# Queries, key copies and a gate product in the first block of a two-block transformer kernel

## The chip, the cores and the metric

One core of one Trainium2 chip runs the whole program. The metric is the device time of one execution in microseconds, as the median over runs.

## What is computed

The reference runs two different two-layer blocks over 256 tokens of width 1024, everything in float32. The change touches the first block alone. One of its layers normalizes the input and projects it to ten parts: queries, keys, values and a gate for attention A (16 heads of 64, a mixture of dilated bands), the same for attention B (8 heads of differential attention), and two output gates. Cut to what matters here:

```python
qa, ka, va, za, qb, kb, vb, zb, ga, gb = split_cols(rms_norm(x) @ w_in)
qa, ka = partial_rope(qa), partial_rope(ka)          # first 16 of 64 columns of a head
ya = dilated_mixture(qa, ka, va) * silu(za)
qb, kb = partial_rope(qb), partial_rope(kb)
yb = subln(diff_attention(qb, kb, vb, lam)) * silu(zb)
x = x + (sigmoid(ga) * (ya @ w_proj_a) + sigmoid(gb) * (yb @ w_proj_b)) @ w_out
```

## The kernel before

Every large product is made in three matmuls per block (`mm3`): both operands are split into a high and a low part. A weight piece (128x1024) is loaded by SP (`raw`), its high part is made on ACT (`hi`), its low part on DVE (`lo`); four split pieces and three raw ones are held. A projection (`proj`) computes 256x512 outputs from four pieces: 16 blocks of three matmuls, eight row chunks by two halves t of the tokens. With `sweep`, all of half 0 comes before half 1; only the first group of a layer does that.

The order of all other work on the engines is written by a small planner. It has a clock that advances by 0.5 at each block (so a *step* of 1.0 is two blocks, six matmuls), and `at(k, fn)` issues `fn` once the clock has gone k steps further. Each engine runs its instructions in the order in which they were issued so, and waits for the semaphores of what it needs.

A layer of the first block makes four groups of eight heads' columns: two for attention A, two for attention B. Per group `qkv` projects queries, keys and values; `attend_a` or `attend_b` then puts the stages of all its heads on the planner, and these run beside the gate's projection and beside the next group's `qkv`. So the queries of the first group have no attention beside them, those of the second and third have attention A's, those of the fourth have attention B's.

Queries and keys leave PSUM through `turned`: ACT copies the half to `tok`, POOL turns its first 16 columns in four operations (`rope`), and `lag` steps later `flip` has PE transpose `tok` in four blocks. The queries' `then` (in `into_stack`) copies each of two row halves on ACT and subtracts on DVE; ACT's second copy and DVE's first subtraction write the same rows and take turns. The keys' `then` (in `into_keys`) does the same into `kh` and `kl`, and at the end four DMAs on SP's queue (`twin`) copy `kh` and `kl` to the other 64 rows. Heads with even number need the first `kh` and the first `kl` copy, the odd ones the second. SP's queue also carries the weight loads.

Attention A handles a head in stages: s (four score matmuls on PE; `s` and its maximum on DVE; `nm`, the scale, on POOL), e (`e`, exponentials on ACT), c (`pc`, the masked product, on DVE in two parts), t (three transposes `pt` on PE, copied by ACT), v (the product with the values into `o`). Behind the fourth and the eighth head follow the reciprocal `rd` on DVE, `rdh` on POOL, the scaled output `yo` on DVE, and the gate product into `sz`. Heads follow each other by 3.2 steps. PSUM buffers for scores, transposes and flips are three in rotation.

Of the kernel before, what the change touches and what calls it, by code (L numbers as in the profile page):

```python
# [16 lines left out]
ALU = mybir.AluOpType  # L17
# [60 lines left out]
def body(ctx: ExitStack, tc: tile.TileContext, I, out, upto=None):  # L78
    nc = tc.nc
    V, S, G, T = nc.vector, nc.scalar, nc.gpsimd, nc.tensor  # L80
# [22 lines left out]
    def tb_(name):  # L103
        o, n = _WHERE[name]
        return tab[:, o - n0:o - n0 + n]
# [118 lines left out]
    rope1 = (tb_("cc").rearrange("p (t d) -> p t d", t=2), tb_("ss").rearrange("p (t d) -> p t d", t=2))  # L224
# [16 lines left out]
    def tick(n=1.0):  # L241
        feed()
        pump(clk[0] + n)
# [54 lines left out]
    def piece():  # L298
        if not splits:
            feed()  # L300
        return splits.popleft()

    def release():
        count["done"] += 1

    def acc2():
        return [ps.tile([128, 512], F32, name="acc", tag="acc", bufs=4) for _ in range(2)]

    def mm3(a, n, lh, c, t, hi, lo, cc, first, last):
        sl = slice(t * 128, (t + 1) * 128)  # L310
        a = a[:, :n]
        T.matmul(a, lh[0][:, c, sl], hi[:, cc, :n], start=first, stop=False)  # L312
        T.matmul(a, lh[0][:, c, sl], lo[:, cc, :n], start=False, stop=False)  # L313
        T.matmul(a, lh[1][:, c, sl], hi[:, cc, :n], start=False, stop=last)  # L314

    def proj(lh, evac, sweep=False):

        acc = acc2()
        if not sweep:
            for c in range(8):  # L320
                if c % 2 == 0:
                    hi, lo, n = piece()
                for t in range(2):
                    mm3(acc[t], n, lh, c, t, hi, lo, c % 2, c == 0, c == 7)
                    if t and c % 2:
                        release()
                    if c == 7:
                        evac(acc[t], t)
                    tick(0.5)
        else:  # L330
            pieces = []
            for t in range(2):
                for c in range(8):
                    if t == 0 and c % 2 == 0:
                        pieces.append(piece())
                    hi, lo, n = pieces[c // 2]
                    mm3(acc[t], n, lh, c, t, hi, lo, c % 2, c == 0, c == 7)
                    if t and c % 2:
                        release()
                    if c == 7:  # L340
                        evac(acc[t], t)
                    tick(0.5)
# [92 lines left out]
    def turned(r, tabs, then, lag):  # L435

        tok = t4k("tok")

        def evac(acc, t):
            S.activation(tok[:, t, :], acc, AF.Copy, scale=factor(r, t))  # L440
            rope(tok[:, t, :], 8, tabs[0][:, t, :], tabs[1][:, t, :])

            def flip():
                p = wk([128, 4, 128], "tp")
                for a in range(4):
                    T.transpose(p[:, a, :], tok[:, t, a * 128:(a + 1) * 128], ident)
                then(p, slice(t * 128, t * 128 + 128), t)
            at(lag, flip)
        return tok, evac

    def halves(i):
        return slice(64 * i, 64 * i + 64), slice(64 - 64 * i, 128 - 64 * i)

    def into_stack(dst, r, tabs):


        def then(p, cols, t):
            for i in range(2):
                a, b = halves(i)
                h = dst[a, i:8:2, cols]  # L460
                S.activation(h, p[a], AF.Copy)
                V.tensor_tensor(out=dst[b, i:8:2, cols], in0=p[a], in1=h.bitcast(F32), op=ALU.subtract)
        return turned(r, tabs, then, 4)

    def into_keys(st, r, tabs):

        def then(p, cols, t):
            if t == 0:
                st["kh"] = act.tile([128, 8, 256], F32R, name="kh", tag="LT", bufs=1)
                st["kl"] = [act.tile([128, 4, 256], F32R, name="kl", tag="Y", bufs=2) for _ in range(2)]  # L470
            for i in range(2):
                a, _ = halves(i)
                h = st["kh"][a, i:8:2, cols]
                S.activation(h, p[a], AF.Copy)
                V.tensor_tensor(out=st["kl"][i][a, :, cols], in0=p[a], in1=h.bitcast(F32), op=ALU.subtract)
            if t == 1:
                def twin():
                    for i in range(2):
                        a, b = halves(i)
                        nc.sync.dma_start(st["kh"][b, i:8:2, :].bitcast(F32), st["kh"][a, i:8:2, :].bitcast(F32))  # L480
                    for i in range(2):
                        a, b = halves(i)
                        nc.sync.dma_start(st["kl"][i][b].bitcast(F32), st["kl"][i][a].bitcast(F32))
                at(0, twin)
        return turned(r, tabs, then, 5.3)[1]
# [135 lines left out]
    def layer1(l, last):  # L621
        lh, r, hr = nxt["lh"], nxt["r"], nxt["hr"]
# [10 lines left out]
        def attend_a(q, k, v, sz, la, g):  # L633
            st = {}

            def s_(h):
                if h % 4 == 0:
                    st["den", h // 4] = tiny(8, "den")
                s, mx = scores(q[:, h, :], k["kh"][:, h, :], k["kl"][h % 2][:, h // 2, :], tb_("ba"))
                nm = tiny(2, "nm")  # L640
                G.tensor_scalar(nm, mx, -0.125, None, op0=ALU.mult)
                st["s", h] = s, nm

            def e_(h):
                s, nm = st.pop(("s", h))
                e = e_tile()
                for j, (a, b) in enumerate(SPL):
                    S.activation(e[:, a:b], s[:, a:b], AF.Exp, bias=nm[:, j:j + 1], scale=0.125)
                st["e", h] = e

            def c_(h):
                den, i, e = st["den", h // 4], h % 4, st.pop(("e", h))
                pc = sm.tile([128, 384], F32, name="pc", tag="pc", bufs=2)
                for j, (a, b) in enumerate(SPL):
                    V.scalar_tensor_tensor(pc[:, a:b], e[:, a:b], 1.0, tb_("ca")[:, a:b], op0=ALU.mult,
                                           op1=ALU.mult, accum_out=den[:, 2 * i + 1 - j:2 * i + 2 - j])
                st["p", h] = pc

            def t_(h):
                st["pt", h] = probs_T(st.pop(("p", h)))  # L660

            def v_(h):
                hh, i = h // 4, h % 4
                if i == 0:
                    st["o"] = wk([128, 4, 2, 64], "o", "o", 1)
                o = st["o"]
                pv_mm(o[:, i, 1, :], o[:, i, 0, :], st.pop(("pt", h)), v, slice(64 * h, 64 * h + 64))
                if i < 3:
                    return
                rd = tiny(8, "rd")  # L670
                V.reciprocal(rd, st["den", hh])
                rdh = tiny(8, "rdh")
                for t in range(2):
                    G.tensor_scalar(by_block(rdh)[:, :, t], by_block(rd)[:, :, t], hr[:, t:t + 1], None, op0=ALU.mult)
                y = half_tile("yo").rearrange("p (t h d) -> p t h d", t=2, h=4)
                V.tensor_tensor(out=y, in0=o.rearrange("p h t d -> p t h d"),
                                in1=rdh.rearrange("p (h t) -> p t h", t=2)[:, :, :, None].to_broadcast([128, 2, 4, 64]),
                                op=ALU.mult)
                z = sz[:, :, 256 * hh:256 * hh + 256]
                G.tensor_tensor(out=z, in0=y.rearrange("p t h d -> p t (h d)"), in1=z, op=ALU.mult)  # L680
                if hh == 1:
                    for t in range(2):
                        at(3.5 + t, lambda t=t: to_lh(la, sz[:, t, :], 4 * g, t))

            for h in range(8):
                queue(3.2, [(d, lambda h=h, fn=fn: fn(h)) for d, fn in
                            ((-0.6, s_), (0.9, e_), (1.1, c_), (3.5, t_), (9.8, v_))])
# [62 lines left out]

        def qkv(first=False):
            q, k = qk_tile([8, 256], F32R), {}
            proj(lh, into_stack(q, r, rope1)[1], sweep=first)
            proj(lh, into_keys(k, r, rope1))
            v = t4k("R", "v")
            proj(lh, into_scaled(v, r))
            return q, k, v

        la = None
        for g in range(2):  # L760
            q, k, v = qkv(g == 0)
# [6 lines left out]
        for g in range(2):  # L768
            q, k, v = qkv()
# [725 lines left out]
    p = wk([128, 512])  # L1495
# [50 lines left out]
```

## Time and profile before

| | us |
|---|---|
| median of three runs | 1749.18 (1749.03 to 1752.28) |
| the profiled execution | 1747.13 |
| its span, first to last instruction | 1745.2 |
| PE busy in the span | 1709.6 |
| mean granted clock of PE | 0.993 of full |

Times within the trace count from the first instruction. A wait is idle time of an engine that ends with the event named. Matmuls overlap: a row's duration is longer than the distance to the next row, and the distance from start to start is what PE spends.

### The profile page before, as it was taken

How to read it: one execution, taken by the hardware profiler on the slowest of the kernel's cores; microseconds unless marked ns; L12 is line 12 of the kernel's file. 1: busy time of each engine (PE TensorE's matmuls, PEld its weight loads, DVE VectorE, ACT ScalarE, POOL GpSimd, SP SyncE). 2: the span in 40 equal slices, each digit the busy share in tenths (PEclk: the TensorE clock that was granted, in tenths of full speed). 3: DMA queues.
4: the chain of work that ended last, by engine and by line, in shares of the span. 5: the costliest groups of instructions: out<-in, count | busy, mean ns of one | idle time of the engine just before them, and what ended most of it. 6: DMA issues, size and time to landing. Idle time of an engine off the chain costs nothing.

```text
span 1745.2 us, 26891 instructions
## 1 busy us (share of the span) xinstructions
PE 1709.6 (98%) x9865; PEld 1485.3 (85%) x9865; DVE 1162.5 (67%) x2109; ACT 1013.2 (58%) x1834; POOL 329.2 (19%) x555
## 2 busy tenths in 40 slices
PE   8999999999999999999999999999999999999998
PEld 7788888888888888898889889998898888889997
DVE  5676776666767666779575676555778685675554
ACT  5666665466666654665676455445665666464443
POOL 2122421031224200342230000000442230010000
PEclk8999999999999999999999999999999999999999
DMA  6655565566554655555233555665555242646664
GB/s 206 195 163 160 158 192 169 168 192 183 169 156 147 192 178 174 169 169 136 88 103 97 186 175 183 191 185 169 170 158 150 76 114 86 198 157 197 184 184 143
DMA packets 158932, 282.27 MB, mean 162 GB/s; under 512 B 20560, under 2 KB 28496, under 8 KB 158800
## 3 DMA queue, kind: packets, MB, share of 16 engines
q1 hardware_dynamic: 157840, 277.83, 52.9%
q0 software_dynamic: 720, 2.62, 0.5%
q8 instruction: 78, 1.28, 0.3%
q14 instruction: 54, 0.44, 0.1%
q10 hardware_dynamic: 240, 0.09, 0.0%
HBM read 270.53 MB, written 1.59 MB: 156 GB/s over the span
## 4 chain that ended last, share of the span: by engine, by line
PE 48%; DVE 6%; ACT 2%; DMA 1%; issue 1%; POOL 0%; DVEq 0%; POOLq 0%; SPq 0%; ACTq 0%
PE acc L314 6%; PE acc L312 6%; PE acc L313 6%; PE acc L353 4%; PE acc L354 4%; PE acc L355 4%; PE facc L313 3%; PE facc L312 3%; PE facc L314 3%; DVE lo L285 2%; PE inv L1178 1%; PE inv L1168 1%; PE tp L371 1%; ACT hi L284 1%; PE pt L507 1%
## 5 line engine op out<-in xcount | busy, mean ns | idle before, releaser
L285 DVE TENSOR_TENSOR lo<-raw,hi 128x1024 fp32r<-128x1024 f32 (+1 forms) x504 | 621.7, 1240 | 339.7 <-ACT hi L284 322.5
L284 ACT ACTIVATE hi<-raw 128x1024 fp32r<-128x1024 f32 (+1 forms) x504 | 528.0, 1053 | 343.6 <-PE acc L314 139.8
L312 PE MATMUL acc<-hi,lhi 128*128 128x512 f32 (+1 forms) x1344 | 551.2, 410 | 2.5 <-ACT lhi L385 2.5
L314 PE MATMUL acc<-hi,llo 128*128 128x512 f32 (+1 forms) x1344 | 526.3, 392 | 0.5 <-DVE llo L388 0.3
L313 PE MATMUL acc<-lo,lhi 128*128 128x512 f32 (+1 forms) x1344 | 524.9, 391 | 0.5 <-DVE lo L285 0.4
L314 PEld LDWEIGHTS acc<-hi,llo 128*128 128x128 f32 x1344 | 253.9, 189 | 57.6 <-DVE llo L388 3.6
L313 PEld LDWEIGHTS acc<-lo,lhi 128*128 128x128 f32 x1344 | 255.6, 190 | 41.5 <-DVE lo L285 2.3
L312 PEld LDWEIGHTS acc<-hi,lhi 128*128 128x128 f32 x1344 | 255.7, 190 | 41.3 <-ACT lhi L385 2.8
L353 PE MATMUL acc<-lhi,hi 128*128 128x256 f32 x832 | 239.0, 287 | 0.0
L355 PE MATMUL acc<-lhi,lo 128*128 128x256 f32 x832 | 235.3, 283 | 0.0
L354 PE MATMUL acc<-llo,hi 128*128 128x256 f32 x832 | 235.2, 283 | 0.0
L353 PEld LDWEIGHTS acc<-lhi,hi 128*128 128x128 f32 x832 | 159.5, 192 | 1.2 <-issue 0.4
L354 PEld LDWEIGHTS acc<-llo,hi 128*128 128x128 f32 x832 | 159.4, 192 | 0.7
L355 PEld LDWEIGHTS acc<-lhi,lo 128*128 128x128 f32 x832 | 159.2, 191 | 0.0
L312 PE MATMUL facc<-hi,fh 128*128 128x512 f32 x256 | 99.8, 390 | 0.0
L313 PE MATMUL facc<-lo,fh 128*128 128x512 f32 x256 | 99.8, 390 | 0.0
L314 PE MATMUL facc<-hi,fl 128*128 128x512 f32 x256 | 99.6, 389 | 0.0
L546 POOL TENSOR_SCALAR pf<-pss 128x1 f32<-128x1 f32 x8 | 3.7, 459 | 468.0 <-ACT pj L856 468.0
L509 ACT ACTIVATE ptS<-pt 128x384 f32<-128x384 f32 x80 | 39.4, 492 | 83.0 <-PE pt L507 82.7
L500 DVE CUSTOM_DVE_ANT_0 s<-sc,tab 128x256 f32<-128x256 f32 x192 | 60.4, 351 | 10.7 <-PE sc L496 9.9
L314 PEld LDWEIGHTS facc<-hi,fl 128*128 128x128 f32 x256 | 48.1, 188 | 10.0
L312 PEld LDWEIGHTS facc<-hi,fh 128*128 128x128 f32 x256 | 48.1, 188 | 9.6
(309 smaller groups left out, 2299.3 us busy)
## 6 DMA issues: line engine op xcount, KB each, us to landing
raw<-in_w_in_dram SPq DMA_DIRECT2D x272, 512.0 KB, 3.7
raw<-in_w_ff_dram SPq DMA_DIRECT2D x128, 512.0 KB, 4.3
raw<-in_w_proj_a_dram SPq DMA_DIRECT2D x16, 512.0 KB, 4.2
raw<-in_w_proj_b_dram SPq DMA_DIRECT2D x16, 512.0 KB, 3.7
raw<-in_w_out_dram SPq DMA_DIRECT2D x16, 512.0 KB, 3.7
raw<-in_w_up_sw_dram SPq DMA_DIRECT2D x16, 512.0 KB, 3.6
raw<-in_w_up_dn_dram SPq DMA_DIRECT2D x16, 512.0 KB, 3.8
raw<-in_w_o_dram SPq DMA_DIRECT2D x16, 512.0 KB, 3.7
```

The source lines that it names most:

```text
L284: S.activation(hi[:, :, :o], raw[:, :, :o], AF.Copy)
L285: V.tensor_tensor(out=lo[:, :, :o], in0=raw[:, :, :o], in1=hi[:, :, :o].bitcast(F32), op=ALU.subtract)
L312: T.matmul(a, lh[0][:, c, sl], hi[:, cc, :n], start=first, stop=False)
L313: T.matmul(a, lh[0][:, c, sl], lo[:, cc, :n], start=False, stop=False)
L314: T.matmul(a, lh[1][:, c, sl], hi[:, cc, :n], start=False, stop=last)
L353: T.matmul(a, hi[:, c % 2, sl], lh[0][:, c, :], start=(c == 0 and m % 2 == 0), stop=False)
L354: T.matmul(a, hi[:, c % 2, sl], lh[1][:, c, :], start=False, stop=False)
L355: T.matmul(a, lo[:, c % 2, sl], lh[0][:, c, :], start=False, stop=(c == 7 and m % 2 == 1))
L371: T.transpose(p[:, a, :], src[:, a * 128:(a + 1) * 128], ident)
L500: V.tensor_tensor_reduce(s[:, a:b], sc[:, a:b], bias[:, a:b], 1.0, FMIN, ALU.add, ALU.max, accum_out=mx[:, j:j + 1])
L507: T.transpose(pt[:, j * 128:(j + 1) * 128], p[:, j * 128:(j + 1) * 128], ident)
L509: S.activation(r, pt, AF.Copy)
```

## The change

Three edits, all in the first block. The query flips are issued six steps behind their evacuation and no longer four, in all four groups of both layers (second block unchanged). The four key copies are issued as kh, kl for the even heads, then kh, kl for the odd ones. The gate product of attention A goes from POOL to DVE.

```diff
-    def into_stack(dst, r, tabs):
+    def into_stack(dst, r, tabs, lag=4):
...
-        return turned(r, tabs, then, 4)
+        return turned(r, tabs, then, lag)
...
                     for i in range(2):
                         a, b = halves(i)
                         nc.sync.dma_start(st["kh"][b, i:8:2, :].bitcast(F32), st["kh"][a, i:8:2, :].bitcast(F32))
-                    for i in range(2):
-                        a, b = halves(i)
                         nc.sync.dma_start(st["kl"][i][b].bitcast(F32), st["kl"][i][a].bitcast(F32))
...
                 z = sz[:, :, 256 * hh:256 * hh + 256]
-                G.tensor_tensor(out=z, in0=y.rearrange("p t h d -> p t (h d)"), in1=z, op=ALU.mult)
+                V.tensor_tensor(out=z, in0=y.rearrange("p t h d -> p t (h d)"), in1=z, op=ALU.mult)
...
             q, k = qk_tile([8, 256], F32R), {}
-            proj(lh, into_stack(q, r, rope1)[1], sweep=first)
+            proj(lh, into_stack(q, r, rope1, 6)[1], sweep=first)
```

## Rows read from the trace of the kernel before

**Rows 1.** The page, busy us, share of the span and instructions of each engine.

```profile
PE 1709.6 (98%) x9865; PEld 1485.3 (85%) x9865; DVE 1162.5 (67%) x2109; ACT 1013.2 (58%) x1834; POOL 329.2 (19%) x555
```

**Rows 2.** PE's waits by releaser, whole span: us in total, times, longest us.

```profile
PE pt L507 <- DVE pc L655: 3.0, 4, 0.8
PE sc L496 <- DMA kl<-kl: 3.0, 3, 1.5
...
PE tp L446 <- POOL tok L430: 2.5, 2, 2.0
```

**Rows 3.** Timeline of PE: start, us, instruction, count [idle before it <- releaser].

```profile
23.26 0.39 PE L314 MATMUL acc<-hi,llo 128*128 128x512 f32 x1
25.69 1.08 PE L446 MATMUL tp<-ident,tok 128*128 128x128 f32 x4 [2.04 <-POOL tok L430]
...
29.40 0.40 PE L313 MATMUL acc<-lo,lhi 128*128 128x512 f32 x1
...
33.28 0.60 PE L446 MATMUL tp<-ident,tok 128*128 128x128 f32 x4
...
35.33 0.39 PE L313 MATMUL acc<-lo,lhi 128*128 128x512 f32 x1
```

**Rows 4.** Windows: busy us of PE, PEld, DVE, ACT, POOL, PEclk, DMA share, GB/s.

```profile
25.70:29.30 3.60, 3.60 (x11) 3.03 (x12) 1.21 (x2) 1.72 (x3) 0.00 (x0) 0.53 0.84 294
59.00:62.00 3.00, 2.98 (x15) 2.52 (x16) 0.71 (x5) 0.71 (x1) 0.23 (x1) 1.00 1.04 349
```

**Rows 5.** Timeline of all engines, the first group's keys.

```profile
51.10 1.41 DVE L475 TENSOR_TENSOR kl<-tp,kh 64x512 fp32r<-64x512 f32 x2 [0.66 <-ACT kh L474]
51.71 2.05 SPq L480 DMA_DIRECT2D kh<-kh  x2
52.55 0.59 ACT L474 ACTIVATE kh<-tp 64x512 fp32r<-64x512 f32 x1 [0.86 <-DVE kl L475]
...
53.81 1.59 SPq L483 DMA_DIRECT2D kl<-kl  x2
...
59.02 0.36 PE L496 MATMUL sc<-kl,qk 128*128 128x256 f32 x1 [1.50 <-DMA kl<-kl]
```

**Rows 6.** Timeline of all engines, first attention A, sixth and seventh head.

```profile
94.03 0.42 DVE L655 SCALAR_TENSOR_TENSOR pc<-e,tab 128x256 f32<-128x256 f32 x1
...
96.30 0.43 DVE L500 CUSTOM_DVE_ANT_0 s<-sc,tab 128x256 f32<-128x256 f32 x1
...
99.38 0.69 DVE L676 TENSOR_TENSOR yo<-o,rdh 128x512 f32<-128x512 f32 x1 [2.32 <-POOL rdh L674]
...
99.99 1.22 DVE L285 TENSOR_TENSOR lo<-raw,hi 128x1024 fp32r<-128x1024 f32 x1
...
100.15 2.17 POOL L680 TENSOR_TENSOR sz<-yo,sz 128x512 f32<-128x512 f32 x1 [0.81 <-DVE yo L676]
...
101.12 1.49 DVE L655 SCALAR_TENSOR_TENSOR pc<-e,tab 128x256 f32<-128x256 f32 x1
...
102.54 0.53 DVE L655 SCALAR_TENSOR_TENSOR pc<-e,tab 128x128 f32<-128x128 f32 x1
102.67 0.79 PE L507 MATMUL pt<-ident,pc 128*128 128x128 f32 x3 [0.72 <-DVE pc L655]
```

**Rows 7.** Timeline of all engines, the second group's query flips.

```profile
89.06 0.69 DVE L462 TENSOR_TENSOR qk<-tp,qk 64x512 fp32r<-64x512 f32 x1 [0.66 <-ACT qk L461]
...
89.90 0.52 PE L507 MATMUL pt<-ident,pc 128*128 128x128 f32 x3
...
91.81 0.69 DVE L462 TENSOR_TENSOR qk<-tp,qk 64x512 fp32r<-64x512 f32 x1 [0.66 <-ACT qk L461]
...
93.27 0.79 ACT L648 ACTIVATE e<-s,nm 128x256 f32<-128x256 f32 x2
```

**Rows 8.** The page's costliest groups: busy us, mean ns | idle before, releaser.

```profile
L284 ACT ACTIVATE hi<-raw 128x1024 fp32r<-128x1024 f32 (+1 forms) x504 | 528.0, 1053 | 343.6 <-PE acc L314 139.8
```

**Rows 9.** Timeline of all engines, attention B's output beside the fourth group's keys.

```profile
213.95 0.35 DVE L743 SCALAR_TENSOR_TENSOR sz<-o,fh,sz 128x128 f32<-128x128 f32 x1 [2.12 <-POOL fh L738]
```

## The prediction

> **What bounds the kernel now.** I read the busy times first: PE is busy for 1709.6 of 1745.2 us, so only PE's waits can be won [rows 1]. Its waits by releaser came next. Three lines lie in the stages that the diff touches: 3.0 us in four waits of the probability transposes (pt) for the masked product pc, 3.0 us in three waits of the score matmuls for the copies of kl, 2.5 us in two waits of the token transposes for POOL's rotary embedding [rows 2]. That is 8.5 us, and the first flip costs more than its idle time shows. The flip of the first group's queries starts at 25.69; the last matmul before it was issued at 23.26, and the next would have followed 0.23 us later, at 23.49. From there to 29.40 PE does four transposes and seven matmuls. The second flip's four transposes and the seven matmuls behind them take 35.33 - 33.28 = 2.05 us [rows 3]. So the wait costs 29.40 - 23.49 - 2.05 = 3.86 us, 2.04 of it idle; the rest is the granted clock, 0.53 from 25.7 to 29.3, that is, mostly the 1.2 GHz level. After the 1.50 us wait at 59.02 it stays at 1.00 [rows 4].
>
> **The change part by part.**
>
> *Queries transposed two steps later, where they waited.* Two steps hold four blocks of three matmuls, 12 x 0.23 = 2.7 us, which is more than the 2.04 us wait. The embedding releases the flip at 25.69 as before, since POOL's order ahead of it is the same, and PE comes there at about 26.2. The key matmuls that now run ahead of the flip need two split weight pieces, which ACT and DVE made without PE's flip. So -3.86 us; the other flip wait, 2.5 - 2.04, goes too: -0.4 us. Kept at both ends of my range.
>
> *Key copies.* SP issues the four copies in program order. The second kh copy can't go before the last ACT copy, 52.55 + 0.59 = 53.14, so the first kl copy goes at 53.81, although DVE had finished its source at 51.10 + 1.41 = 52.51 [rows 5]. In the new order it goes at about 52.5, 1.3 us earlier, and with one copy of 256 KB less ahead of it. What waits for it, the first head's score at 59.02, had waited 1.50 us; the other two waits share 1.5 us. I take all 3.0 us as won (least: 2.4, if the landing moves only by the issue in the longest wait). The second kh copy goes about 0.7 us later; the second head's score is 3.2 steps behind the first's, at least 3.2 x 6 x 0.23 = 4.4 us, which hides it.
>
> *Gate product on DVE.* It runs eight times, twice per call of `attend_a`. The one behind the fourth head is beside a PE wait. POOL's product takes 2.17 us there, and DVE's first pc beside it takes 1.49 us instead of 0.42: 1.07 us lost on the path to the transposes at 102.67 [rows 6]. On DVE the product costs about half of a split's 1.22 us (128x512 for 128x1024, the same operation): 0.61 us, in the same queue ahead of the same pc. That gains 0.46. But POOL then starts the second half's four rotary operations as soon as rdh is done, beside product, split and pc. The second part of pc, with half the elements of the first, takes 0.53 us where one of them runs beside it, some 0.2 more than it should; two such meetings give nearly all of the gain back, one gives half. I take -0.25, between -0.5 and +0.5, for each of four windows: -1.0. The Trainium skill ("SBUF - State Buffer", Who interferes with whom) says that a DVE operation with two SBUF inputs and a GpSimd operation that reads SBUF exclude each other for the whole instruction; the 1.49 us agrees. By that rule the four rotary operations, which POOL works off ahead of rdh between s and yo, some 1.5 us together, could all fall in DVE's way, 1.0 us more than the product's move gains; the sum below would then be some 5 us higher, 1752, at the upper edge of no change, and its chance is in that case. The other four products stand behind the eighth head, where PE has no such wait: 0, hidden by DVE's idle third.
>
> *Queries transposed two steps later, where they did not wait.* The shift holds for all eight groups, and six of them have the previous group's attention running beside them. More than PE's transposes moves: each flip brings two ACT copies (0.6 us, as for the keys [rows 5]) and two DVE subtractions (0.69) that wait for each other in turn, and holds up what is queued behind them on ACT and DVE [rows 7]. In the second group they now end at 91.81 + 0.69 = 92.50, then come two weight splits, the sixth head's pc between them at 94.03, and the seventh head's score evacuation s at 96.30 [rows 6]. After the change the first split and the sixth head's exponential go ahead of the flips, the flips stand directly before the second split. The fifth head's transposes, now at 89.90, come at about 88.9 without two flips of 0.36 us ahead of them; behind them stand the copy of their result (some 0.5 us) and the exponential (0.79), so ACT turns to the flips at about 90.5. One flip takes 2 x (0.6 + 0.69) and the handovers, 2.7 us; pc comes between the two, 0.6; the second takes 2.0, as its first copy runs beside DVE's work for the first: 5.3 us, to 95.8. ACT is through its last copy 0.7 us earlier, at 95.1; its half of the split (1.05) [rows 8] ends at 96.1, DVE's (1.22) at about 97.3. So s comes about 1.0 us later. Nothing behind it has slack: s, its scale on POOL, the first half's embedding on POOL, rdh, then yo, for which DVE sat idle for 2.32 us, split, pc, and the transposes at 102.67 that PE already waits for. So they start 1.0 us later, in each of four windows: +4.0 us, bounds 0 (the chain catches up) and +6 (1.5 each, if ACT's handovers are slower). The idle time there grows a little more than that: the fifth head's transposes at 89.90 start right after the flip's subtraction at 89.06 frees their buffer, and no longer have to [rows 7], so PE comes some 0.25 us earlier.
>
> The last group of each layer has the other attention beside it. There the output scaling waits 2.12 us on DVE for POOL [rows 9], and the subtractions, which stood ahead of it, now stand behind it; the third head's exponentials, its transposes and the key flips follow. No row prices that; the nearest is those 2.12 us: between 0 and +2.1 in each of two windows, I take the middle: +2.0 together.
>
> *Sum*: -3.9 - 0.4 - 3.0 - 1.0 + 4.0 + 2.0 = -2.3 us. The profiled execution took 1747.13 us, so 1744.8; the median of the runs shown lies 2.05 us above it (1749.18), which gives about **1747 us**. Less than 0.2% (3.5 us) can't be told from no change here.
>
> **The rivals.** *The later flips cost little.* The chain could catch up before the seventh head's transposes, because ACT and DVE have idle time (DVE a third). Then the gains stand alone: -8.3 us, 1741. For it: the won waits are in the trace, the loss is not. Against: the chain to 102.67 runs through two in-order queues without a gap. It decides when the loss of the moved flips is under 4.8 us in all (I have 6.0).
>
> *The clock falls with the longer wait.* This one ends on the other side. The wait of the seventh head's transposes grows from 0.75 us (3.0 in four [rows 2]) to about 2.0 (0.75 + 1.0 + 0.25). Behind 2.04 us the clock fell, behind 1.50 it did not [rows 3 to 5]. A fall costs 3.86 - 2.04 = 1.8 us. In all four windows: 4 x 1.8 = 7.2, and -2.3 + 7.2 = +4.9 us, 1754; it decides from four falls on, or three with half a microsecond of other loss. For it: the row at 25.7; against: the estimate lies between the two waits that the trace shows, and four of four would have to fall. The Trainium skill ("TensorE: Matmul & The Clock Gate", Part 1: The HAM clock gate) says that the clock is gated by how busy PE has been and knows two levels; the row at 25.7 agrees.
>
> *The change does nothing for the copies*, because the landing is set by other transfers: DMA share is 1.04 from 59 to 62 [rows 4]. Then +3.0 on the sum, 1750, still no change.
>
> **How the numbers follow.** Losses of 4.8 to 11.8 us against 8.3 won: within 0.2%, chance 0.45 (the copies that don't help among them), and in its middle the forecast, 1747, own range 1745.7 to 1752.7. Losses under 4.8: faster, 0.33, since 6.0 is taken between wide bounds and lies only 1.2 above the line. Losses over 11.8, by the clock: slower, 0.22. The range for 8 in 10 reaches from the gains alone, 1741, to all four falls, 1754.
>
> **What would show it.** Right: no wait before the first flip and clock 1.00 from 20 to 40 us; no wait for kl; pc beside no POOL product at 0.42; but waits of pt for pc of 1.5 to 2.2 us, four times, s of the seventh head about 1 us later against the score on PE, and new waits in the last group of each layer. Wrong: pt waits no longer than 0.8 us (then the first rival), a granted clock of about 0.5 behind them (the second), or a wait for split weights behind 25 us.

## The result and the profile after

The changed kernel takes 1762.33 us (median of 6 runs, 1757.82 to 1767.89) against 1750.84 (6 runs of the kernel before, 1749.03 to 1752.28): ratio 1.0067, 95% interval 1.0053 to 1.0080. It is 11.7 us slower (9.3 to 14.0); no change was forecast, at -2.3 us. Below, a ratio is turned into us of 1750. The ratios are those on record, taken over the runs of both kernels; they need not equal the quotient of the two medians beside them (for e14 1.0018 against 1.0009). Line numbers behind line 481 are two lower than before, since the diff takes two lines away.

First the page's busy times of the changed kernel, then PE's waits over its whole span (us in total, times, longest); they answer to [rows 1, 2].

```profile
PE 1710.7 (97%) x9865; PEld 1483.5 (84%) x9865; DVE 1163.6 (66%) x2117; ACT 1010.9 (57%) x1834; POOL 317.2 (18%) x547
```

```profile
PE pt L505 <- DVE pc L653: 6.9, 5, 1.7
...
PE pt L505 <- DVE pc L714: 4.2, 4, 1.3
...
PE acc L313 <- DVE lo L285: 2.8, 4, 0.8
...
PE tp L446 <- POOL tok L430: 1.3, 3, 0.7
```

PE does the same work, so the loss is waiting and clock. The waits of the scores for kl are down to one of 0.43 us (three, 3.0 us, before). The waits for attention A's pc grew from 3.0 to 6.9 us. Those for attention B's pc (4.2) and most of those for split weights (2.8) are new.

To see where the time goes, one counts the matmuls of one line and compares when the k-th of them starts in the two traces (L314 with hi and llo, 1344 of them, k the same program point in both). Changed minus before, in stretches of the time of before:

| stretch of before, us | what lies there | forecast | measured |
|---|---|---|---|
| 18 to 30 | first query flip | -3.9 | -4.3 |
| 30 to 54 | second flip, keys of the first group | 0 | +7.2 |
| 54 to 61 | first score behind the key copies | -1.5 | -1.7 |
| 80 to 106, 130 to 165, 400 to 450, 484 to 530 | second and third group, beside attention A | +3.0 | +0.9, +0.9, +0.9, +2.1 |
| 372 to 384 | first flip of layer 2 | -0.4 | -0.7 |
| 180 to 252, 530 to 592 | fourth group, beside attention B | +0.5 | +2.5, +2.5 |
| 592 to 727 | end of layer 2 | 0 | +1.2 |
| 727 to the end | second block, program unchanged | 0 | +4.6 |

The fourth group's forecast is +2.0 less the two kl waits of 0.73; attention A's is +4.0 less 1.0. The last line can't be pinned on the change: the profiled execution of before (1747.13) is 3.7 us under its median here, and of the 15 experiments below, which all have the same second block, 14 are later there than before's too, by 0.2 to 5.2 us.

The start, on PE (timeline; start, duration, instruction, idle before it and what ended it) and in windows (PE, PEld, DVE, ACT, POOL busy, PEclk, DMA share, GB/s) of the changed kernel:

```profile
26.07 0.66 PE L446 MATMUL tp<-ident,tok 128*128 128x128 f32 x4 [0.25 <-POOL tok L430]
...
42.73 0.49 PE L312 MATMUL acc<-hi,lhi 128*128 128x512 f32 x1 [0.68 <-ACT hi L284]
...
43.99 0.50 PE L313 MATMUL acc<-lo,lhi 128*128 128x512 f32 x1 [0.77 <-DVE lo L285]
...
45.39 1.11 PE L446 MATMUL tp<-ident,tok 128*128 128x128 f32 x4 [0.67 <-POOL tok L430]
...
48.17 1.11 PE L446 MATMUL tp<-ident,tok 128*128 128x128 f32 x4 [0.39 <-POOL tok L430]
```

```profile
40.00:43.50 3.50, 2.55 (x10) 1.27 (x8) 2.16 (x3) 2.68 (x5) 0.03 (x1) 1.00 0.48 145
43.50:50.30 6.80, 5.25 (x16) 3.78 (x17) 4.13 (x5) 5.52 (x8) 4.12 (x8) 0.60 0.46 126
```

The first flip waits 0.25 us at full clock (2.04 us and the clock at 0.53 behind it in [rows 3, 4]). But 16 us later the split weights are late, then the keys' own flips, and the clock is granted at 0.60. ACT and DVE show why (timeline of the same kernel), with one row of before's ACT below:

```profile
29.32 1.06 ACT L284 ACTIVATE hi<-raw 128x1024 fp32r<-128x1024 f32 x1 [4.75 <-DMA raw<-in_w_in_dram]
...
35.03 1.28 ACT L166 ACT_TABLE_LOAD   x1
35.24 0.16 DVE L195 CAST pf<-pi 128x2 f32<-128x2 int32 x1
...
38.74 0.22 DVE L164 SCALAR_TENSOR_TENSOR lv<-lv 128x64 f32<-128x64 f32 x1
...
39.43 0.20 ACT L166 ACTIVATE le<-le 128x4 f32<-128x4 f32 x1 [3.12 <-DVE lv L164]
39.66 0.59 ACT L461 ACTIVATE qk<-tp 64x512 fp32r<-64x512 f32 x1
...
41.62 1.06 ACT L284 ACTIVATE hi<-raw 128x1024 fp32r<-128x1024 f32 x1
```

```profile
40.92 1.04 ACT L284 ACTIVATE hi<-raw 128x1024 fp32r<-128x1024 f32 x1
```

The table work (the lambda factors, L164 to L168, and the angles of the second block's rotary embedding, L195 to L216) is queued on ACT and DVE here: ACT loads a function table and waits 3.12 us for DVE, which works off the angles (from 35.24) and a weight split before it comes to the products for the lambda factors (38.74). The second flip's copies, two steps later than before, now stand behind that, and the next split behind them, at 41.62; PE waits for it at 42.73. In the kernel before the same piece's split started at 40.92: PE came 4 us sooner, its weights did not.

The first attention A window (all engines; answers to [rows 6]):

```profile
98.45 0.42 DVE L498 CUSTOM_DVE_ANT_0 s<-sc,tab 128x256 f32<-128x256 f32 x1
...
101.52 0.69 DVE L674 TENSOR_TENSOR yo<-o,rdh 128x512 f32<-128x512 f32 x1 [2.32 <-POOL rdh L672]
102.25 0.77 DVE L678 TENSOR_TENSOR sz<-yo,sz 128x512 f32<-128x512 f32 x1
...
102.27 0.43 PE L511 MATMUL o<-v,ptS 128*128 128x64 f32 x2 [0.23 <-DVE yo L674]
102.55 0.79 POOL L430 TENSOR_TENSOR tok<-ra,rb 128x128 f32<-128x128 f32 x1
102.94 1.48 DVE L285 TENSOR_TENSOR lo<-raw,hi 128x1024 fp32r<-128x1024 f32 x1
104.34 0.41 DVE L653 SCALAR_TENSOR_TENSOR pc<-e,tab 128x256 f32<-128x256 f32 x1
...
104.81 0.55 PE L505 MATMUL pt<-ident,pc 128*128 128x128 f32 x3 [1.66 <-DVE pc L653]
```

pc runs at 0.41 instead of 1.49, as forecast. But s comes at 98.45 against 96.30; less the 0.7 us that this point of PE's program is later anyway, s is 1.47 us late, and PE waits 1.66 us for pc instead of 0.72, with a new wait of 0.23 for yo.

The fourth group beside attention B, changed kernel, and one row of before's ACT for the exponential concerned:

```profile
213.49 1.13 DVE L741 SCALAR_TENSOR_TENSOR sz<-o,fh,sz 128x128 f32<-128x128 f32 x4 [2.12 <-POOL fh L736]
...
215.36 1.21 ACT L461 ACTIVATE qk<-tp 64x512 fp32r<-64x512 f32 x2 [3.35 <-DVE qk L462]
...
217.43 0.59 ACT L461 ACTIVATE qk<-tp 64x512 fp32r<-64x512 f32 x1 [0.86 <-DVE qk L462]
...
219.01 0.49 ACT L702 ACTIVATE e<-s,nm 128x256 f32<-128x256 f32 x1
...
221.76 0.63 DVE L714 SCALAR_TENSOR_TENSOR pc<-e,rdb 128x256 f32<-128x256 f32 x1
...
222.54 0.89 PE L505 MATMUL pt<-ident,pc 128*128 128x128 f32 x3 [1.33 <-DVE pc L714]
```

```profile
211.90 0.49 ACT L704 ACTIVATE e<-s,nm 128x256 f32<-128x256 f32 x1
```

The output scaling on DVE waits 2.12 us for POOL as before [rows 9], but the flips' subtractions are queued behind it now. On ACT a flip's copy waits 3.35 us for the first of them, and the flips' copies stand ahead of the exponentials: from 211.90 they move to 219.01 (some 4.5 us of it by this, 2.6 by PE being later), pc behind them, and PE waits 1.33 us where it had not.

### The profile page after: what moved, and what is told of

It reads as the page before. It is cut to its first block, busy times and chain, and to the rows that moved or that the text cites. A ratio compares the mean times of both kernels' runs of the same rounds, so it can differ in the third digit from the quotient of the medians.

```text
span 1761.0 us, 26864 instructions
## 1 busy us (share of the span) xinstructions
PE 1710.7 (97%) x9865; PEld 1483.5 (84%) x9865; DVE 1163.6 (66%) x2117; ACT 1010.9 (57%) x1834; POOL 317.2 (18%) x547
## 4 chain that ended last, share of the span: by engine, by line
PE 45%; DVE 6%; DMA 3%; ACT 2%; issue 2%; POOL 1%; SPq 0%; DVEq 0%; POOLq 0%; ACTq 0%
PE acc L314 5%; PE acc L312 5%; PE acc L313 5%; PE acc L353 4%; PE acc L354 3%; PE acc L355 3%; PE facc L312 3%; PE facc L313 3%; PE facc L314 3%; DVE lo L285 3%; DMA raw<-in_w_in_dram 1%; PE inv L1176 1%; PE inv L1166 1%; ACT hi L284 1%; PE tp L371 1%
## 5 line engine op out<-in xcount | busy, mean ns | idle before, releaser
L314 PE MATMUL acc<-hi,llo 128*128 128x512 f32 (+1 forms) x1344 | 525.6, 391 | 1.0 <-DVE llo L388 0.9
L314 PEld LDWEIGHTS acc<-hi,llo 128*128 128x128 f32 x1344 | 253.4, 189 | 57.7 <-DVE llo L388 3.8
L314 PE MATMUL facc<-hi,fl 128*128 128x512 f32 x256 | 99.6, 389 | 0.0
L498 DVE CUSTOM_DVE_ANT_0 s<-sc,tab 128x256 f32<-128x256 f32 x192 | 60.3, 351 | 10.3 <-PE sc L494 9.6
L314 PEld LDWEIGHTS facc<-hi,fl 128*128 128x128 f32 x256 | 48.1, 188 | 10.2
```

What stands on the lines that cost most here:

```text
L498: V.tensor_tensor_reduce(s[:, a:b], sc[:, a:b], bias[:, a:b], 1.0, FMIN, ALU.add, ALU.max, accum_out=mx[:, j:j + 1])
```

## The experiments

All times are medians, each beside the kernel before on the same chip.

**One part at a time.** The lag alone, the product alone, the copies alone, and the last two together:

```diff
-            proj(lh, into_stack(q, r, rope1)[1], sweep=first)
+            proj(lh, into_stack(q, r, rope1, 6)[1], sweep=first)
...
-                G.tensor_tensor(out=z, in0=y.rearrange("p t h d -> p t (h d)"), in1=z, op=ALU.mult)
+                V.tensor_tensor(out=z, in0=y.rearrange("p t h d -> p t (h d)"), in1=z, op=ALU.mult)
...
-                    for i in range(2):
-                        a, b = halves(i)
```

Lag alone. 

> Only the queries' transposes two steps later, in all eight groups; copies and product as before. Theory A (the lag pays for everything): in the trace of the changed kernel the 4.6 us that the first flip won were lost again between 40 and 55 us, 7 us in all, because the second flip's copies and subtractions then queue behind table work on ACT and DVE; each attention A window lost about 0.9 us (one of the four 2.1), each fourth group 2.45. Without the product's gain and the copies' gain: +2.3 + 5 + 4.9 = +12 us, 1763, and up to 1767 if the 4.6 us that the unchanged second block lost belong to it. Theory B (the product on DVE costs the attention A windows, the lag only the start and the fourth groups): +2.3 + 4.9 = +7 us, 1758.

Measured 1761.22 against 1750.05, ratio 1.0069 (1.0053 to 1.0084): +12 us. Theory A; the lag is the whole loss.

Product alone. 

> Only the gate product on DVE. Theory A: the stretch from yo to the end of pc took 3.37 instead of 3.62 us in the changed kernel, so -0.25 us in each of four windows, -1.0 us, 1750. Theory B: the product costs DVE what the windows lost, +0.9 each and more, +4 to +5 us, 1755.

1749.20 against 1750.05, 0.9990 (0.9981 to 0.9999): -1.7 us (-3.3 to -0.2). Matmul by matmul its trace wins 0.26, 0.27, 0.25 and 0.27 us in the four windows. Theory B falls.

Copies alone. 

> Only the order of the key copies. Theory A (as predicted): the three waits of the scores for kl, 3.0 us, go: 1748. Theory C (the landing is set by other transfers): no change, 1751.

1750.62 against 1750.05, 1.0005 (0.9995 to 1.0015): no gain. But theory C is wrong about the reason. PE's waits in its trace, and ACT's way to the first head's exponential:

```profile
55.90 0.36 PE L494 MATMUL sc<-kl,qk 128*128 128x256 f32 x1 [0.45 <-DMA kl<-kl]
62.95 0.52 PE L505 MATMUL pt<-ident,pc 128*128 128x128 f32 x3 [0.38 <-DVE pc L653]
...
244.97 0.91 PE L505 MATMUL pt<-ident,pc 128*128 128x128 f32 x3 [0.47 <-DVE pc L714]
...
588.97 0.91 PE L505 MATMUL pt<-ident,pc 128*128 128x128 f32 x3 [1.03 <-DVE pc L714]
```

```profile
59.45 1.06 ACT L284 ACTIVATE hi<-raw 128x1024 fp32r<-128x1024 f32 x1 [4.11 <-DMA raw<-in_w_in_dram]
60.52 1.28 ACT L646 ACT_TABLE_LOAD   x1
61.82 0.80 ACT L646 ACTIVATE e<-s,nm 128x256 f32<-128x256 f32 x2
```

The three kl waits did go, but for 0.45 us. Each time PE then came to the same head's transposes before pc did: matmul by matmul the first wait won 1.1 us and 0.6 was lost by 66 us, the second won 1.0 and 0.8 was lost by 247, the third won 1.0 and 1.4 was lost by 592; 1.7 more went between 180 and 205 us, behind waits of 0.39 and 0.80. For the first head the rows name the chain: its exponential stands in ACT's queue behind a weight split that waits 4.11 us for its transfer and behind a table load, so a score 1.1 us earlier against PE's program did not bring pc forward. For the other two no single link stands out.

Product and copies. 

> Product and copies together, the transposes at their old steps. Theory A: -1.0 - 3.0 = -4 us, 1747, faster than before by 0.2%. Theory B: +4.5 - 3 = +1.5, 1752.

1748.10 against 1750.05, 0.9990 (0.9980 to 1.0000): -1.7 us, the product's share; the -4 of theory A is just outside. The copies add nothing here either: waits of 0.77, 0.49 and 0.51 us for pc stand behind the removed ones.

**The lag by groups.** `qkv` gets a lag for each group, here for the first group alone (e5); e6 gives 6 to that group's first token half and 4 to its second, e7 gives 6 to the second and third group, e8 to the fourth:

```diff
-            q, k, v = qkv(g == 0)
+            q, k, v = qkv(g == 0, (6, 4)[g])
...
-            q, k, v = qkv()
+            q, k, v = qkv(False, (4, 4)[g])
```

First group. 

> Later transposes in the first group of each layer alone, both token halves. As predicted, -3.9 and -0.4 us: 1746. Theory A (the second half's copies and subtractions now stand behind the table work, and the weight split that follows behind them): -4.6 won at the first transpose and about 5.5 given back between 40 and 50 us, -0.6 in the second layer: +0 to +1 us, 1750 to 1751, with waits of the matmuls for hi and lo near 43 us and a granted clock of about 0.6 behind them.

1749.43 against 1748.22, 1.0002 (0.9994 to 1.0011): +0.3 us. Theory A; the forecast's -4.3 is lost.

First token half alone. 

> As the run before, but only the first token half two steps later; the second half stays at four steps, so that its copies and subtractions stand ahead of the table work, as in the kernel before. Theory A: the gain stays, -4.6 and up to -0.6: 1745 to 1746, no waits for hi or lo between 40 and 50 us, clock 1.00. Theory W (it is the weight stream itself that comes too late for a PE that runs 4 us ahead): the same loss as with both halves, 1750 to 1751.

1748.64 against 1748.22, 1.0000 (0.9991 to 1.0010): nothing won, against my theory A, and not told apart from both halves. Its PE waits:

```profile
40.59 0.50 PE L313 MATMUL acc<-lo,lhi 128*128 128x512 f32 x1 [1.24 <-DVE lo L285]
45.03 0.66 PE L446 MATMUL tp<-ident,tok 128*128 128x128 f32 x4 [0.57 <-POOL tok L430]
47.80 0.66 PE L446 MATMUL tp<-ident,tok 128*128 128x128 f32 x4 [1.42 <-POOL tok L430]
59.66 0.36 PE L496 MATMUL sc<-kl,qk 128*128 128x256 f32 x1 [1.80 <-DMA kl<-kl]
```

So the order of copies and table work is not enough: a weight split stands behind the angles on DVE (lo at 39.32), the next one on ACT behind the lambda factors (41.27), and everything after these is as late as before. The next four runs take the table work away.

Second and third group. 

> Later transposes in the second and third group of each layer alone, which have attention A beside them; product on POOL. As predicted (the seventh head's score evacuation 1.0 us later, four times): +4, 1754. Theory A, from the trace of the run with the lag alone: +3.0, +2.6, +1.4 and +1.4 in the four windows, where the clock fell behind the longer waits: +8.4, 1758 to 1759.

1756.52 against 1748.22, 1.0044 (1.0030 to 1.0059): +7.7 us (5.2 to 10.3), nearer to theory A. Two of its four windows, PE and windows:

```profile
103.69 0.79 PE L507 MATMUL pt<-ident,pc 128*128 128x128 f32 x3 [1.66 <-DVE pc L655]
...
452.57 0.79 PE L507 MATMUL pt<-ident,pc 128*128 128x128 f32 x3 [1.66 <-DVE pc L655]
```

```profile
103.70:107.00 3.30, 3.28 (x17) 2.60 (x18) 2.20 (x8) 1.14 (x3) 2.54 (x5) 1.00 0.50 156
...
452.60:456.00 3.40, 3.38 (x12) 2.52 (x13) 2.31 (x8) 1.28 (x4) 2.50 (x5) 0.69 0.44 153
```

The wait is 1.66 us in all four; behind two of them the clock falls, which costs 1.6 and 1.3 us more: net +1.1, +1.1, +2.7, +2.4. This execution (1758.90) lies 2.4 us above its kernel's median, and it loses outside these windows too, each time behind a wait for kl with a clock fall: 2.1 us at 57 us (2.03 waited, 1.50 before) and 2.9 at 235 (2.00 waited, 0.73 before). That the edit causes these is not shown; the traces with the same groups at three and five steps (below) wait 1.5 us at most at the first place and 0.7 at the second.

Fourth group. 

> Later transposes in the fourth group of each layer alone, beside attention B. As predicted +2.0 (0 to 4.2): 1752. Theory A: 2.45 to 3.3 in each layer: +5 to +6.5, 1755 to 1756.5, with a wait of the probability transposes for pc of 1.3 us where there was none.

1754.23 against 1748.22, 1.0027 (1.0015 to 1.0040): +4.7 us (2.6 to 7.0). PE's new and longer waits in layer 1:

```profile
219.62 0.88 PE L507 MATMUL pt<-ident,pc 128*128 128x128 f32 x3 [1.33 <-DVE pc L716]
233.90 0.36 PE L496 MATMUL sc<-kl,qk 128*128 128x256 f32 x1 [1.67 <-DMA kl<-kl]
```

1.33 for pc and 1.67 instead of 0.73 for kl are 2.27 us, and layer 2 has the same pair: 4.5. The three groups add up to +0.3 + 7.7 + 4.7 = +12.7 us for the lag's +12.

**Is it the table work?** The lambda factors and the angles are computed later, at 141 and 319 us instead of 40 and 36, from a buffer that is free until the second block. e9 is e5 with that, the loads where they were (steps 4.9 and 4.7, the work 70 and 177 steps behind); e10 postpones the loads too (steps 68 and 175, the work 7.3 behind); e11 is e10 without the lag, e12 is e10 with product and copies:

```diff
-        at(k, lambda load=load: at(7.3, load()))
+        at(k, lambda d=d, load=load: at(d, load()))
```

> First group of each layer two steps later (both halves), and the table work (the lambda factors and the angles of the second block) computed later, about 100 us behind where it stood and at about 290 us; its loads stay where they were, into a buffer that is free until the second block. Keeping the second half's copies ahead of the table work alone had given nothing (a wait for lo of 1.24 us at 40.6 us, for the keys' transposes of 0.57 and 1.42, for kl 1.80). Theory T (the chain on ACT and DVE from the weight piece that lands at 29 us to the piece made at 41 us is as long as before because the table work stays in it): without it most of the 4.6 us is kept, -3 to -4.5 us against before. Theory W (what is late is the weight piece that lands at 29 us, for which ACT idles 3.5 to 4.8 us): -1 at most.

1744.62 against 1749.83, 0.9966 (0.9955 to 0.9978): -5.9 us. PE's only waits for another engine or a transfer from 24 to 100 us, and the windows in which the changed kernel lost:

```profile
25.07 0.66 PE L446 MATMUL tp<-ident,tok 128*128 128x128 f32 x4 [0.92 <-POOL tok L430]
...
96.57 0.79 PE L507 MATMUL pt<-ident,pc 128*128 128x128 f32 x3 [0.72 <-DVE pc L655]
```

```profile
40.00:43.50 3.50, 3.35 (x19) 2.54 (x19) 3.31 (x4) 2.60 (x3) 2.77 (x3) 1.00 0.60 180
43.50:50.30 6.80, 6.80 (x32) 5.59 (x31) 4.51 (x6) 4.62 (x7) 0.00 (x0) 1.00 0.95 279
```

No wait for weights or keys, no wait for kl either, clock 1.00. Theory T.

> As the run before, and the table work's loads postponed with it, so that five small transfers less stand ahead of the weight pieces on SP. Theory T: as the run before, -3 to -4.5. Theory W: the piece lands earlier than 29 us and the gain is kept here alone, -3 to -4.5, with no idle ACT at 25 to 29 us.

1744.93 against 1749.83, 0.9971 (0.9962 to 0.9980): -5.1 us. The transfers were not what was late; theory W falls.

> Control: the kernel before with the table work and its loads postponed, transposes at four steps. PE waits for nothing of the table work there, so 0 (within 1 us) by both theories; whatever it gains is not the later transposes'.

1749.13 against 1749.83, 0.9997 (0.9986 to 1.0009): no change. Later flips alone gain nothing (e5), postponing alone gains nothing, both together gain 5. The control's trace is not empty, though: its wait for kl at 59 us is gone (-1.7), and the postponed work costs PE time where it stands now. In e10 that is 1.2 us beside the second attention A, where the wait for pc grows from 0.72 to 1.67 us, and 1.2 at about 325 us. So -5.1 is what is left after these; no run tries a better place.

> The first group two steps later, table work and loads postponed, with the gate product on DVE and the key copies in the new order: the run of the postponed loads, -0.9 for the product, 0 to -1 for the copies: -4 to -6 us by theory T or W if that run keeps its gain.

1744.46 against 1749.83, 0.9966 (0.9954 to 0.9979): -5.9 us. It beats both kernels, and so does e9 without product and copies: these add nothing that can be measured on top.

**Other shifts beside attention A.** Second and third group at three and at five steps, and three steps in e12:

> The opposite shift: transposes of the second and third group at three steps instead of four, all else as before. Theory S (what counts is how many of the two transposes' subtractions stand on DVE between the sixth and the seventh head's score evacuation: none at three steps, one at four, two at five and six): s of the seventh head comes about 1 us earlier against its score, the waits of 0.7 to 0.8 us for pc become less than 0.2, -2 to -3 us. Theory P (the wait for pc in the kernel before has nothing to do with the transposes: the splits and POOL's rotary embedding set it): waits as before, 0.

1752.75 against 1749.71, 1.0014 (1.0004 to 1.0024): +2.4 us, slower. Theory S falls, and so does P: the waits grow to between 1.26 and 1.31 us.

> Transposes of the second and third group at five steps. Theory S: as at six steps, two subtraction pairs between the two score evacuations: waits of about 1.6 us, +5 to +8 us. Theory D (the loss grows with the shift): half of the 7.7 us measured at six steps, +3 to +4, waits of about 1.2 us.

1751.32 against 1749.71, 1.0018 (1.0004 to 1.0031): +3.2 us, theory D's size, but with waits of 1.46 to 1.56 us, nearer to S's 1.6. First windows of both, the run at three steps first:

```profile
101.11 0.79 PE L507 MATMUL pt<-ident,pc 128*128 128x128 f32 x3 [1.26 <-DVE pc L655]
```

```profile
102.16 0.79 PE L507 MATMUL pt<-ident,pc 128*128 128x128 f32 x3 [1.49 <-DVE pc L655]
```

What holds at every shift is the time of the seventh head's score evacuation s, measured against PE's program at the same point (the matmul that starts at 92.1 in before): 0.55 us later at three steps, 0.77 at five, 1.45 at six. From there to the end of the window PE loses 0.55, 0.77 and 1.45 us; it has gained some 0.3 just before, so the net is 0.25, 0.4 and 1.1. In e13's trace the clock also fell behind the fourth wait, in e14's behind none; the rest of +2.4 and +3.2 is not resolved. At three steps it is the sixth head's s that the flips delay, and its exponential and pc behind it; at five and six they delay the seventh's. Four steps is the best of these.

> The best run so far (first group two steps later, table work and loads postponed, product on DVE, copies in the new order; -5.9 against before) with the second and third group at three steps. Theory S: 2 to 3 us less again, -8 to -9. Theory P: -6.

1745.73 against 1749.71, 0.9979 (0.9969 to 0.9988): -3.7 us, 2.2 less gained than without the three steps. Neither S nor P.

## Why the prediction was wrong, point by point

**First flip: the failed step.** I forecast -3.86 and -0.4 because the matmuls that run ahead of the flip "need two split weight pieces, which ACT and DVE made without PE's flip". That was true, and PE was 4.3 us ahead at 30 us (against an execution of before in which the clock had fallen there). The step did not ask which chain sets the pieces that follow, and kept the gain at both ends of the range. That chain is ACT's and DVE's: a piece lands at 29 us, and the table work between it and the split that starts at about 41 us is in their queues whatever PE does. PE was ahead for some 15 us, then waited for weights, for keys and (6.8 us at 0.60) for its clock. Alone, the step is worth +0.3 us; with the table work moved, -5.1 and -5.9. "A wait for split weights behind 25 us" stood among the signs of a wrong forecast, without a chance of its own.

**Key copies: wrong.** Forecast -3.0, measured +0.9 (-0.9 to +2.6). The copies land earlier as forecast. What failed is taking a wait of PE at its length: pc did not come earlier with the score, and PE met it at the same head's transposes (0.38, 0.47 and 1.03 us). For the first head ACT's queue shows why, a split that waits 4.11 us for its weights ahead of the exponential; for the others the cause stays open.

**Flips beside attention A: mechanism right, term too small.** Forecast +1.0 each, from an s 1.0 us late; s is 1.45 us late, and less the 0.3 us by which PE comes earlier this makes 1.1 each; a wait of 0.23 to 0.30 us for yo, which I had not listed, is part of it. Of the rest of the 7.7 us the profiled execution shows 2.9 as the second rival: the clock fell behind two of the four waits in e7, two in e1 and one in the changed kernel. The wait is 1.66 us, not 2.0.

**Fourth group: term too small.** Forecast +2.0, 0 to 4.2; measured +4.7. The subtractions do queue behind the scaling's wait, and the cost goes on through ACT (a copy waits 3.35 us for them, the exponentials stand behind the copies, 1.33 us at pc), and the delay goes on into the keys, whose copies land 0.94 us later against the score.

**Gate product: right.** Forecast -0.25 each; 0.25 to 0.27 in the trace, -1.7 (-3.3 to -0.2) in the times. The Trainium skill's rule on DVE and GpSimd ("SBUF - State Buffer", Who interferes with whom), with all four rotary operations in DVE's way, would by the prediction's estimate have cost 1.0 us a window more than the move gains. The trace agrees with the rule, not with that many meetings: the first two rotary operations ran beside yo, which reads o from PSUM, and only the last two met the product and the split. There the last took 0.79 us (0.46 in the first half), the product 0.77 (0.69 behind the eighth head) and the split 1.48 for 1.22.

By their single runs the parts add up to +0.3 + 7.7 + 4.7 - 1.7 + 0.9 = +11.9 us; the whole measured +11.7. Against the forecast's terms that is 4.6 us for the first flips, 3.9 for the copies, 3.7 beside attention A, 2.7 beside attention B and -0.7 for the product. Of the rivals, the clock came in part and "does nothing for the copies" came true for another reason; each was priced as if the rest held, and they came together. Open stays the +1.2 us at the end of layer 2, which the lag alone does not show, and how much of the second block's +4.6 us is more than the spread between executions.

## What to carry to other kernels

A wait removed from the bounding engine is worth its length only up to the next point where that engine meets a chain it does not drive: follow the other engines' queues past the wait to the next such point, and look for one-time setup work and for splits that wait for their transfers in them. In these in-order queues a moved step is paid by what it now stands ahead of, so move it only in the place where it waits (here the first group alone, with the setup work out of the way), not by one constant for all places.

## What the runs showed of the hardware

The granted clock does not follow from a wait's length alone. Behind the 1.66 us wait for pc it fell to between 0.52 and 0.69 of full in five of twelve windows (e1, e7 and the changed kernel) and stayed at 1.00 in seven; in e13 it fell behind one of four waits of about 1.3 us, in e14 behind none of four of about 1.5. Behind the first flip it fell after 2.04 us in the kernel before, 3.05 in e4, 3.61 in e14 and 3.67 in e8, but not after 2.04 in e3, 2.44 in e2 and e13, 2.80 in e7 and 2.87 in e11. A fall there or in a window cost 1.2 to 1.8 us. So part of my -3.86 was a cost that not every execution pays.
